# A two-layer decoder trunk on one core: value products gathered, MLP chunks interleaved, gates moved behind later queries

## The chip, the cores and the metric

The kernel runs on one core of a Trainium2 chip. The metric is the device time of one execution in microseconds; lower is better. TensorE (PE) does matrix products into PSUM; its weight loads are listed as PEld. VectorE (DVE), ScalarE (ACT) and GpSimd (POOL) do the elementwise work, and SyncE (SP) issues most DMAs.

## The reference, cut to what matters

Two pre-norm residual layers act on x, 256 tokens by 2048 features, in float32. Layer 0 is grouped-query attention (32 query heads in 4 groups, head dimension 64) over a sliding window of 128 with sinks. Layer 1 is native sparse attention in three branches: compressed keys, selected blocks (with 256 tokens all four blocks are selected) and a window of 512, mixed by sigmoid gates. The compressed keys and values come from a small MLP.

```python
def compress(k, pos, w1, w2):
    blocks = k[:, idx] + pos            # 15 blocks of 32 tokens
    return jax.nn.gelu(blocks @ w1) @ w2
...
    q, kc, vc, ks, vs, kw, vw, gates, z = jnp.split(h @ w_in, ...)
    o = g[0] * o_cmp + g[1] * o_slc + g[2] * o_win
    return (o * jax.nn.silu(z)) @ w_out
```

## The kernel before, in words

**Projections.** The weights stream through in chunks of 128x1024 floats (512 KB), one chunk a step; `steps` holds all of them in order. `load` brings a chunk into one of 4 `raw` buffers four steps ahead. `split`, two steps ahead, makes two float32r parts of it: ACT copies `w_hi`, DVE subtracts to get `w_lo` (3 buffers each). A "tok" step then makes 12 products of 512 columns into the two accumulators `acc0` and `acc1` (one for each half of the tokens), and a "feat" step makes 8 pairs of 512 and 256 columns. A block of 8 tok steps, or two blocks of 4 feat steps, gives 512 output columns, and a `post_...` function takes them out of PSUM. There are 3 PSUM banks with the tag `acc`.

**Order of the steps.** Layer 0 has keys and values, then for each group g its queries (`post_q`) and its gate (`add_z`, `post_z`), then the output projection. Layer 1 has the compressed branch's keys and values (`post_kc`), the selected branch's (`post_kv`), the first MLP (`add_mlp(0)`, 4 chunks of 8 products with 256 columns), the window branch's keys and values, the second MLP (`add_mlp(1)`), the branch gates, then queries and gate of groups 0, 1, 2, 3, then the output projection.

**Attention in the background.** A unit is a group g and a half of the tokens t. Its front transposes the queries, makes scores and softmax; its back transposes the probabilities (`p_transposed`, into `pt` tiles), makes the value products and calls `finalize`. `pipeline` zips the front of one unit with the back of the unit before. After each half step `background` runs pieces of these generators as long as their prices are covered by a credit that grows by `rate` for each half step. A generator that has to wait yields None, which ends that turn.

**The value products.** `pv_pair` makes two products, one for the upper and one for the lower 64 output partitions of the bank `pv`; each is two instructions in the trace, so a pair is four. In layer 1 a unit with t=0 has 2 blocks (so 2 pairs), and one with t=1 has 4. Every pair is issued when the block after it has been transposed. `finalize` waits until the gate of its group is done, multiplies the gate tile `u` by `pv` straight from PSUM, and makes the two parts `aT_hi` and `aT_lo` that the output projection reads.

**The order on the engines.** Nothing is issued when it is called. `Plan.record` collects all operations, and `Plan.order` replays them with estimated prices: on each engine the earliest recorded operation that is ready goes first. The accumulating products get `LAST`, so they fill PE wherever nothing else is ready; the splits get `FIRST`. `together` keeps products side by side on PE. The order that comes out is fixed; on the chip the engines then wait on semaphores. All operations carry the helper's line, L217, so the views are read by tile names.

Of the kernel before, what the change touches and what calls it, by code (L numbers as in the profile page):

```python
# [12 lines left out]
F32 = mybir.dt.float32  # L13
F32R = mybir.dt.float32r
# [6 lines left out]
P = 128  # L21
# [4 lines left out]
NG = 4  # L26
# [313 lines left out]
def trunk(ctx: ExitStack, tc: tile.TileContext, x, final_norm_w, a_w_in, a_w_out, b_w_in, kc_pos, kc_w1, kc_w2, vc_pos, vc_w1, vc_w2,  # L340
# [9 lines left out]
    def acc_bank(name):  # L350
        return pp.tile([P, NB], F32, tag="acc", name=name, bufs=3)
# [10 lines left out]
    def copy(out, in_, scale=1.0):  # L362
        return ACT.activation(out, in_, AF.Copy, scale=scale)
# [272 lines left out]

    def post_q(layer, g):
        def post(t, ps):
            q = sb.tile([P, 2, NB], F32, tag="qs", name="q", bufs=2)[:, 0]
            copy(q, ps, scale=rq[layer][:, t:t + 1])  # L640
            rope(q.rearrange("p (h d) -> p h d", d=HD), t, HPG)
            qs[layer, g, t] = q
            flags.add(("q", layer, g, t))
        return post
# [27 lines left out]

    def post_kv(layer, kT, offs, vt):
        def post(t, ps):
            both = sb.tile([P, 2 * HPG, HD], F32, tag="qs", name="k32", bufs=2)
            k32 = both[:, 0:NG]
            copy(k32.rearrange("p h d -> p (h d)"), ps[:, 0:256], scale=rms[layer][:, t:t + 1])
            DVE.tensor_scalar(vt()[:, t, :], ps[:, 256:512], rms[layer][:, t:t + 1], None, op0=OP.mult)
            rope(k32, t, NG)
            twice = both[:, HPG:2 * HPG].rearrange("p (g a) d -> p g a d", a=2)  # L680
            copy(twice, k32[:, :, None, :].to_broadcast([P, NG, 2, HD]))
            urgent.append(keys_to(kT(), twice, offs[t]))
        return post
# [4 lines left out]
    def post_z(layer, g, part):  # L688
        def post(b, ps):
            if part == b == 0:  # L690
                us[layer, g] = sb.tile([P, 4, S], F32, tag="u", name="u", bufs=2)
            u = us[layer, g][:, 2 * part + b, :]
            side = sb.tile([P, S], F32, tag="q32", name="side", bufs=2)
            copy(side, ps[:, S:2 * S])
            DVE.tensor_tensor(u, ps[:, 0:S], side, op=OP.add)
            if b == 0:
                return
            u = us[layer, g][:, 2 * part:2 * part + 2, :]
            DVE.tensor_tensor(u, u, rbc[:, None, :].to_broadcast([P, 2, S]), op=OP.mult)
            th = sb.tile([P, 2, S], F32, tag="q32", name="th", bufs=2)  # L700
            ACT.activation(th, u, AF.Tanh)
            DVE.scalar_tensor_tensor(u, th, 1.0, u, op0=OP.add, op1=OP.mult)
            if part == 1:
                flags.add(("z", layer, g))
        return post

    def add_z(w, width, col0, layer, g, act):
        for part in range(2):
            add_steps(w, width, col0 + g * NB + part * NB // 2, "feat", act, post_z(layer, g, part))

    def new_aT():
        return (sb.tile([P, KT, S], F32R, tag="aT_hi", name="aT_hi"),
                sb.tile([P, KT, S], F32R, tag="aT_lo", name="aT_lo"))

    def finalize(layer, g, t, pv, aT):
        while ("z", layer, g) not in flags:
            yield None
        u = us[layer, g][:, :, t * P:(t + 1) * P]
        DVE.tensor_tensor(u, u, pv, op=OP.mult)
        hi = aT[0][:, 4 * g:4 * g + 4, t * P:(t + 1) * P]  # L720
        copy(hi, u)
        DVE.tensor_sub(aT[1][:, 4 * g:4 * g + 4, t * P:(t + 1) * P], u, hi)
        flags.add(("a", layer, g, t))
        yield 0.0
# [6 lines left out]
            copy(out, in_)  # L731

    def pt_tile():
        return sb.tile([P, 4, P], F32, tag="pt", name="pt", bufs=4)

    def pv_pair(pv, v, pts, first, last):
        plan.together([PE.matmul(pv[par * HD:(par + 1) * HD], v, pts[par], start=first, stop=last)
                       for par in range(2)])

    def a_scores(g, t, kT, qT, par, sm, nm, den):  # L740
        n = (t + 1) * P
# [53 lines left out]

    def pv_blocks(sms, blocks, pv, close):

        prev = None
        for k, (br, off, v) in enumerate(blocks):
            pts = yield from p_transposed(sms, br, off, k)  # L800
            if prev:
                pv_pair(pv, *prev, prev_first, False)
                yield 900.0
            prev, prev_first = (v, pts), k == 0
        pv_pair(pv, *prev, prev_first, close)
        yield 900.0

    def zip_pieces(a, b):

# [24 lines left out]
    def a_back(g, t, vt, sms, aT):  # L834
        pv = pv_bank()
        gs = slice(g * HD, (g + 1) * HD)
        if t == 0:
            yield from pv_blocks(sms, [(0, 0, vt[:, 0, gs])], pv, True)
        else:
            pts = [[], []]  # L840
            for par in range(2):
                tb = t_bank("pT")
                for i in range(4):
                    PE.transpose(tb[:, i, :], sms[par][0][:, i, 0:P], ident)
                for k in range(2):
                    pt = pt_tile()
                    DVE.tensor_tensor(pt, tb, part[:, k, None, :].to_broadcast([P, 4, P]), op=OP.mult)
                    pts[k].append(pt)
                yield 440.0
            for k in range(2):  # L850
                pv_pair(pv, vt[:, 1 - k, gs], pts[k], k == 0, k == 1)
                yield 900.0
        yield from finalize(0, g, t, pv, aT)

    def pipeline(units, front, back):
# [101 lines left out]
    def post_kc(t, ps):  # L957
        if t == 0:
            b_tiles()
        s = sb.tile([P, 2 * NG, 2, HD], F32, tag="qs", name="kcdup", bufs=2)  # L960
        DVE.tensor_scalar(s, ps.rearrange("p (a d) -> p a d", d=HD)[:, :, None, :].to_broadcast([P, 2 * NG, 2, HD]),
                          rms[1][:, t:t + 1], None, op0=OP.mult)
        urgent.append(kc_gen(t, s))
# [45 lines left out]

    def mlp_tail(kind, ps):  # L1010
        H = room(CH)
        copy(H[0:122], ps[0:122, 0:CH])
        yield 0.0
        tb = t_bank("hid")
        for ut in range(2):
# [15 lines left out]
        copy(c32, tb[0:60, 0, 0:HD])  # L1031
        yield 220.0
        if kind == 0:
            s = sb.tile([P, 1024], F32R, tag="qs", name="cstack", bufs=2)[0:60, 0:256].rearrange(
                "p (a b d) -> p a b d", a=2, b=2)
            src = c32[:, None, :].to_broadcast([60, 2, HD])
            copy(s[:, 0], src)
# [10 lines left out]
        else:  # L1048
            yield 0.0
            tb = t_bank("vsel")  # L1050
            for g in range(NG):
                for b in range(2):
                    PE.matmul(tb[b * HD:(b + 1) * HD, g, 0:HD], mlp["sel"][:, g, :], c32, start=True, stop=True)
            vh = sb.tile([P, 1024], F32R, tag="qs", name="vh", bufs=2)[:, 0:256].rearrange("p (g d) -> p g d", g=NG)
            copy(vh, tb[:, :, 0:HD])
            for b in range(2):
                for hl in range(2):
# [6 lines left out]
            yield 900.0  # L1064
            flags.add("vcmp")

    def add_mlp(kind):
        box = {}

        def mk(i):  # L1070
            st = Step()
            st.cols = 1024
            st.dma = w_dma(W1[kind][0], i * 4 * P, 4, 0, CH, CH)

            def half(b):
                if i == 0 and b == 0:
                    need(("X", kind))
                    box["ps"] = acc_bank("mlp")
                X = mlp["X", kind]
                ps = box["ps"]  # L1080
                for kk in (2 * b, 2 * b + 1):
                    kt = 4 * i + kk
                    for pi, w_ in enumerate((st.hi, st.lo)):
                        PE.matmul(ps[0:122, 0:CH], X[:, kt, :], w_[:, kk * CH:(kk + 1) * CH],
                                  start=kt == 0 and pi == 0, stop=kt == KT - 1 and pi == 1)
                if i == 3 and b == 1:
                    urgent.append(mlp_tail(kind, ps))
            st.halves = [lambda: half(0), lambda: half(1)]
            return st
        for i in range(4):  # L1090
            steps.append(mk(i))
# [43 lines left out]
    def b_add(col, kind, post, before=None):  # L1135
        add_steps(b_w_in[0], B_IN, col, kind, of_hT(hT_b), post, before=before)

    aTB = []
    b_add(2048, "tok", post_kc, before=b_before)
    b_add(2560, "tok", post_kv(1, lambda: lay["kT"], (128, 0), lambda: lay["vs"]))  # L1140
    add_mlp(0)
    b_add(3072, "tok", post_kv(1, lambda: lay["kT"], (272, 400), lambda: lay["vw"]))
    add_mlp(1)
    add_gates()
    for g in range(NG):
        b_add(g * NB, "tok", post_q(1, g))
        add_z(b_w_in[0], B_IN, 3680, 1, g, hT_b)
    nB = len(steps)

    def b_scores(g, t, qT, par, sm, nm, den, sc):  # L1150
# [71 lines left out]
    def b_back(g, t, ctx_):  # L1222
# [13 lines left out]
        tb = t_bank("pcT", F32R)  # L1236
        for i in range(4):
            PE.transpose(tb[:, i, :], pc[:, 2 * i:2 * i + 2].rearrange("p a b c d -> p (a b c d)"), identr)
        pcT = sb.tile([P, 4, P], F32R, tag="pt", name="pcT", bufs=4)
        copy(pcT, tb.bitcast(F32))  # L1240
        yield 230.0
        yield 0.0
# [60 lines left out]
    hT_pair(0, hT0, 0)  # L1303
    for i in range(AHEAD):
        split(steps[i])
    rates = [(0, 450.0), (nA, 900.0), (nA + 8, 600.0), (nA_out, 700.0), (nB, 1200.0)]
    for i, st in enumerate(steps):
        for start, r in rates:
            if i == start:
# [77 lines left out]
```

## Time and profile before

| | before |
|---|---|
| median of 3 runs | 786.74 us (786.48 to 786.99) |
| the profiled execution | 786.12 us, its span 784.4 us |
| granted TensorE clock, mean | 0.998 |
| PE busy | 769.8 us, 98% of the span |
| DVE busy | 561.3 us, 72% |
| ACT busy | 465.8 us, 59% |
| POOL busy | 121.7 us, 16% |

Busy times of PE overlap with the drain of each product, so a product of 512 columns is listed as 0.39 us long while products start about every 0.23 us. The time that a piece of PE work costs is read from start to start.

### The profile page before, as it was taken

To read this page: it belongs to the slowest core of one execution; us is meant where nothing else is said; L and a number is where in the kernel's file an instruction comes from. 1 tells how busy PE (TensorE), PEld (TensorE's weight loads), DVE (VectorE), ACT (ScalarE), POOL (GpSimd) and SP (SyncE) were. 2 spreads that over 40 slices of the span, in tenths; PEclk is the share of its full clock that TensorE was granted. 3 is DMA by queue.
4 is the path that set the end of the run, shared out by engine and by line. 5 is a ranking of instruction groups with operands and counts; after the bars stand their busy time and mean duration, and the time that the engine had idled before them with its cause. 6 is when DMAs were issued, how large, how long until landed. Compare 5 with 4: busy or idle time off the path is not lost.

```text
span 784.4 us, 11578 instructions
## 1 busy us (share of the span) xinstructions
PE 769.8 (98%) x3988; PEld 621.3 (79%) x3988; DVE 561.3 (72%) x1159; ACT 465.8 (59%) x940; POOL 121.7 (16%) x170
## 2 busy tenths in 40 slices
PE   8999999999999999999999999999999999999995
PEld 5888788788787888888788887787778768768884
DVE  6649859779589555566756489769949879965562
ACT  6857557466475544445746486577557758744442
POOL 1111213023022000020101102121111031111110
PEclk9999999999999999999999999999999999999999
DMA  9763654564544565665767653444534453355642
GB/s 326 239 201 121 188 162 136 165 183 134 170 153 155 168 195 183 186 199 162 221 200 217 180 161 108 134 136 113 153 103 128 146 139 108 113 183 171 199 168 107
DMA packets 86474, 129.73 MB, mean 165 GB/s; under 512 B 6322, under 2 KB 43233, under 8 KB 86288
## 3 DMA queue, kind: packets, MB, share of 16 engines
q1 hardware_dynamic: 85648, 127.16, 53.3%
q0 software_dynamic: 336, 1.29, 0.4%
q8 instruction: 31, 0.51, 0.3%
q10 hardware_dynamic: 432, 0.56, 0.2%
q14 instruction: 27, 0.22, 0.1%
HBM read 126.89 MB, written 2.10 MB: 164 GB/s over the span
## 4 chain that ended last, share of the span: by engine, by line
PE 90%; DVE 4%; issue 2%; ACT 1%; DMA 1%; POOL 1%; ACTq 0%; POOLq 0%; DVEq 0%
PE acc L217 74%; PE pv L217 5%; PE s L217 4%; PE pT L217 4%; DVE sm L217 1%; DVE w_lo L217 1%; PE qT L217 1%; ACT w_hi L217 1%; PE xT L217 1%; DMA raw<-in_a_w_in 1%; PE gates L217 1%; DVE u L217 0%; PE pcT L217 0%; POOL rope L217 0%; PE mlp L217 0%
## 5 line engine op out<-in xcount | busy, mean ns | idle before, releaser
L217 DVE TENSOR_TENSOR w_lo<-raw,w_hi 128x1024 fp32r<-128x1024 f32 (+1 forms) x231 | 292.8, 1270 | 159.3 <-ACT w_hi L217 152.3
L217 ACT ACTIVATE w_hi<-raw 128x1024 fp32r<-128x1024 f32 (+1 forms) x231 | 241.5, 1049 | 188.9 <-PE acc L217 150.7
L217 PE MATMUL acc<-w_hi,hT 128*128 128x512 f32 x768 | 243.6, 394 | 1.6 <-ACT w_hi L217 1.6
L217 PE MATMUL acc<-hT,w_hi 128*128 128x512 f32 x512 | 186.2, 398 | 0.0
L217 PEld LDWEIGHTS acc<-w_hi,hT 128*128 128x128 f32 x768 | 141.8, 188 | 34.1 <-ACT w_hi L217 5.3
L217 PE MATMUL acc<-w_lo,hT 128*128 128x512 f32 x384 | 150.7, 394 | 0.0
L217 PE MATMUL acc<-hT,w_lo 128*128 128x256 f32 x512 | 145.0, 285 | 0.0
L217 PEld LDWEIGHTS acc<-hT,w_hi 128*128 128x128 f32 x512 | 96.2, 188 | 22.0 <-issue 4.1
L217 PEld LDWEIGHTS acc<-hT,w_lo 128*128 128x128 f32 x512 | 96.7, 189 | 1.5 <-issue 0.8
L217 PE MATMUL acc<-w_hi,aT_lo 128*128 128x512 f32 x236 | 92.4, 391 | 0.0
L217 PE MATMUL acc<-w_hi,aT_hi 128*128 128x512 f32 x236 | 92.1, 392 | 0.0
L217 PE MATMUL acc<-w_lo,aT_hi 128*128 128x512 f32 x236 | 92.0, 391 | 0.0
L217 PEld LDWEIGHTS acc<-w_lo,hT 128*128 128x128 f32 x384 | 72.2, 188 | 16.4 <-issue 2.4
L217 ACT ACTIVATE sm<-sm,nmb 128x128 f32<-128x128 f32 (+1 forms) x128 | 56.8, 444 | 17.9 <-DVE nmb L217 15.7
L217 PEld LDWEIGHTS acc<-w_lo,aT_hi 128*128 128x128 f32 x236 | 44.3, 188 | 11.3 <-issue 2.4
L217 PEld LDWEIGHTS acc<-w_hi,aT_hi 128*128 128x128 f32 x236 | 44.3, 188 | 9.7 <-ACT w_hi L217 0.8
L217 PEld LDWEIGHTS acc<-w_hi,aT_lo 128*128 128x128 f32 x236 | 44.3, 188 | 8.9
L217 POOL TENSOR_TENSOR sm<-sm,denb 128x512 f32<-128x512 f32 (+1 forms) x16 | 28.8, 1798 | 140.9 <-DVE denb L217 71.4
L217 DVE CUSTOM_DVE_ANT_0 sm<-s,mask 128x128 f32<-128x128 f32 (+1 forms) x128 | 43.7, 349 | 9.2 <-PE s L217 9.0
L217 PEld LDWEIGHTS pT<-ident,sm 128*128 128x128 f32 x256 | 30.0, 140 | 13.7 <-issue 5.4
L217 PE MATMUL pT<-ident,sm 128*128 128x128 f32 x256 | 38.8, 276 | 1.2 <-DVE sm L217 0.8
L217 PE MATMUL s<-kTB,qT 128*128 128x272 f32 x192 | 37.8, 292 | 0.0
(186 smaller groups left out, 854.9 us busy)
## 6 DMA issues: line engine op xcount, KB each, us to landing
raw<-in_b_w_in SPq DMA_DIRECT2D x88, 512.0 KB, 3.7
raw<-in_a_w_in SPq DMA_DIRECT2D x71, 512.0 KB, 3.7
raw<-in_a_w_out SPq DMA_DIRECT2D x32, 512.0 KB, 4.4
raw<-in_b_w_out SPq DMA_DIRECT2D x32, 512.0 KB, 4.4
x<-in_x SPq DMA_DIRECT2D x8, 256.0 KB, 6.7
raw<-in_b_cmp_k_w SPq DMA_DIRECT2D x4, 512.0 KB, 3.7
raw<-in_b_cmp_v_w SPq DMA_DIRECT2D x4, 512.0 KB, 4.0
out<-x SPq DMA_DIRECT2D x4, 512.0 KB, 3.2
```

Source lines behind the costliest of these rows:

```text
L217: return getattr(eng.real, method)(*[real(a) for a in args], **{k: real(a) for k, a in kw.items()})
```

## The change

Five things change, and the rest of the diff is buffers that follow from them.

1. `pv_products` takes all blocks of a unit at once, after all of them are transposed; `pt` gets 8 buffers for 4.
2. The 8 MLP chunks alternate with the 8 chunks of the window branch's keys and values (`mixed`); both MLPs share one PSUM bank, a half each.
3. The last gates of layer 1 move: q0 z0 q1 z1 q2 q3 z2 z3 in place of q0 z0 q1 z1 q2 z2 q3 z3.
4. `finalize` no longer waits for a gate: if it isn't done, ACT copies `pv` into a tile `o`, and `gated` runs when the gate is.
5. The rate in layer 1's projections is 750 for 700. Queries get tiles of their own (`q`, 4 buffers), other users of `qs` move to `sm`, and the DMA scratch is set to 8192.

```diff
+            q = sb.tile([P, NB], F32, tag="q", name="q", bufs=4)
...
+                urgent.extend(gated(layer, g, *held) for held in late.pop((layer, g), []))
...
     def finalize(layer, g, t, pv, aT):
-        while ("z", layer, g) not in flags:
-            yield None
+        if ("z", layer, g) not in flags:
+            o = sb.tile([P, NB], F32, tag="q", name="o", bufs=4).rearrange("p (a b) -> p a b", a=4)
+            copy(o, pv)
+            late.setdefault((layer, g), []).append((t, o, aT))
+            yield 0.0
+            return
+        yield from gated(layer, g, t, pv, aT)
+
+    def gated(layer, g, t, pv, aT):
...
+    def pv_products(pv, blocks, close):
+        plan.together([PE.matmul(pv[par * HD:(par + 1) * HD], v, pts[par], start=k == 0,
+                                 stop=close and k == len(blocks) - 1)
+                       for k, (v, pts) in enumerate(blocks) for par in range(2)])
...
     def pv_blocks(sms, blocks, pv, close):
-        prev = None
+        done = []
         for k, (br, off, v) in enumerate(blocks):
             pts = yield from p_transposed(sms, br, off, k)
-            if prev:
-                pv_pair(pv, *prev, prev_first, False)
-                yield 900.0
-            prev, prev_first = (v, pts), k == 0
-        pv_pair(pv, *prev, prev_first, close)
-        yield 900.0
+            done.append((v, pts))
+        yield 0.0
+        pv_products(pv, done, close)
+        yield 800.0 * len(blocks)
...
+                    if kind == 0:
+                        mlp_bank["ps"] = acc_bank("mlp")
...
-    add_mlp(0)
-    b_add(3072, "tok", post_kv(1, lambda: lay["kT"], (272, 400), lambda: lay["vw"]))
-    add_mlp(1)
+    mixed(lambda: b_add(3072, "tok", post_kv(1, lambda: lay["kT"], (272, 400), lambda: lay["vw"])),
+          lambda: (add_mlp(0), add_mlp(1)))
     add_gates()
-    for g in range(NG):
-        b_add(g * NB, "tok", post_q(1, g))
-        add_z(b_w_in[0], B_IN, 3680, 1, g, hT_b)
+    for kind, g in ("q", 0), ("z", 0), ("q", 1), ("z", 1), ("q", 2), ("q", 3), ("z", 2), ("z", 3):
+        if kind == "q":
+            b_add(g * NB, "tok", post_q(1, g))
+        else:
+            add_z(b_w_in[0], B_IN, 3680, 1, g, hT_b)
...
-    rates = [(0, 450.0), (nA, 900.0), (nA + 8, 600.0), (nA_out, 700.0), (nB, 1200.0)]
+    rates = [(0, 450.0), (nA, 900.0), (nA + 8, 600.0), (nA_out, 750.0), (nB, 1200.0)]
...
-    nc = _bacc.Bacc("TRN2", target_bir_lowering=False, num_devices=1)
+    nc = _bacc.Bacc("TRN2", target_bir_lowering=False, num_devices=1, dynamic_dma_scratch_size=8192)
```

## Rows read from the trace of the kernel before

**Rows 1.** The page: busy time of each engine, and the chain that ended last.
```profile
PE 769.8 (98%) x3988; PEld 621.3 (79%) x3988; DVE 561.3 (72%) x1159; ACT 465.8 (59%) x940; POOL 121.7 (16%) x170
...
PE 90%; DVE 4%; issue 2%; ACT 1%; DMA 1%; POOL 1%; ACTq 0%; POOLq 0%; DVEq 0%
```

**Rows 2.** Waits of PE alone: total us, times, longest.
```profile
PE mlp L217 <- DVE w_lo L217: 1.0, 2, 0.5
...
PE pT L217 <- DVE sm L217: 0.8, 3, 0.3
PE kT L217 <- ACT k L217: 0.7, 2, 0.4
```

**Rows 3.** Windows: busy us (instructions) by engine, clock, DMA share, GB/s.
```profile
380.00:422.00 42.00, 40.26 (x232) 33.95 (x231) 26.39 (x32) 25.92 (x40) 7.25 (x16) 1.00 0.72 212
450.00:710.00 260.00, 258.86 (x1435) 203.08 (x1434) 212.50 (x583) 172.15 (x422) 45.88 (x54) 1.00 0.46 132
```

**Rows 4.** Timeline of PE, layer 1: start us, length, form, count in a row.
```profile
509.03 0.62 PE L217 MATMUL acc<-w_hi,hT 128*128 128x512 f32 x2
509.49 0.40 PE L217 MATMUL acc<-w_lo,hT 128*128 128x512 f32 x1
509.81 1.08 PE L217 MATMUL pv<-pt,vw 128*64 128x512 f32 x4
510.82 0.74 PE L217 MATMUL acc<-w_hi,hT 128*128 128x512 f32 x2
511.40 0.40 PE L217 MATMUL acc<-w_lo,hT 128*128 128x512 f32 x1
```

**Rows 5.** Timeline of PE, layer 0, a unit with t=1.
```profile
91.87 0.39 PE L217 MATMUL acc<-w_lo,hT 128*128 128x512 f32 x1
92.18 1.94 PE L217 MATMUL pv<-pt,vA 128*64 128x512 f32 x8
94.05 0.74 PE L217 MATMUL acc<-w_hi,hT 128*128 128x512 f32 x2
94.63 0.40 PE L217 MATMUL acc<-w_lo,hT 128*128 128x512 f32 x1
```

**Rows 6.** The tile pv: its value products in layer 1.
```profile
L217 PE MATMUL pv<-pt,vs x48: 592/618/644, 476.5 to 697.2; 128*64 128x512 f32 x48
...
L217 PE MATMUL pv<-pt,vw x48: 592/618/644, 479.3 to 702.8; 128*64 128x512 f32 x48
```

**Rows 7.** Timeline of PE in the first MLP; in brackets the wait.
```profile
384.51 0.28 PE L217 MATMUL mlp<-w_hi,X 128*122 128x256 f32 x1
385.29 0.38 PE L217 MATMUL mlp<-w_lo,X 128*122 128x256 f32 x1 [0.50 <-DVE w_lo L217]
385.51 0.28 PE L217 MATMUL mlp<-w_hi,X 128*122 128x256 f32 x1
385.62 0.28 PE L217 MATMUL mlp<-w_lo,X 128*122 128x256 f32 x1
```

**Rows 8.** Groups by line, 372 to 425 us: the splits (busy us, mean ns).
```profile
L217 DVE TENSOR_TENSOR w_lo<-raw,w_hi 128x1024 fp32r<-128x1024 f32 x20 | 24.5, 1235 | 15.5 <-ACT w_hi L217 15.5
L217 ACT ACTIVATE w_hi<-raw 128x1024 fp32r<-128x1024 f32 x21 | 21.9, 1057 | 14.3 <-PE acc L217 9.1 <-PE gates L217 2.1 <-DVE room L217 1.6
```

**Rows 9.** Timeline of PE: one wait of keys, one of probabilities.
```profile
390.27 0.66 PE L217 MATMUL kT<-ident,k 128*128 128x128 f32 x4 [0.42 <-ACT k L217]
...
488.52 0.40 PE L217 MATMUL acc<-w_lo,hT 128*128 128x512 f32 x1
489.22 0.66 PE L217 MATMUL pT<-ident,sm 128*128 128x128 f32 x4 [0.31 <-DVE sm L217]
```

**Rows 10.** Groups by line, 450 to 710 us: splits and evacuations.
```profile
L217 DVE TENSOR_TENSOR w_lo<-raw,w_hi 128x1024 fp32r<-128x1024 f32 x62 | 84.3, 1360 | 22.6 <-ACT w_hi L217 19.8 <-PE acc L217 2.3
...
L217 ACT ACTIVATE pt<-pT 128x512 f32<-128x512 f32 x24 | 14.0, 586 | 9.1 <-PE pT L217 9.1
```

**Rows 11.** Chunk loads issued between 372 and 425 us: KB each, median us to landing.
```profile
raw<-in_b_w_in SPq DMA_DIRECT2D x14, 512.0 KB, 4.6
```

More of the change, by code (lines that the diff above doesn't have):

```diff
@@ L638, in post @@
         def post(t, ps):
-            q = sb.tile([P, 2, NB], F32, tag="qs", name="q", bufs=2)[:, 0]
+            q = sb.tile([P, NB], F32, tag="q", name="q", bufs=4)
             copy(q, ps, scale=rq[layer][:, t:t + 1])
@@ L674, in post @@
         def post(t, ps):
-            both = sb.tile([P, 2 * HPG, HD], F32, tag="qs", name="k32", bufs=2)
+            both = sb.tile([P, 2 * HPG, HD], F32, tag="sm", name="k32", bufs=4)
             k32 = both[:, 0:NG]
@@ L713, in new_aT @@
                 sb.tile([P, KT, S], F32R, tag="aT_lo", name="aT_lo"))
+    late = {}
     def finalize(layer, g, t, pv, aT):
-        while ("z", layer, g) not in flags:
-            yield None
+        if ("z", layer, g) not in flags:
[6 more added lines that the diff above has]
+    def gated(layer, g, t, pv, aT):
         u = us[layer, g][:, :, t * P:(t + 1) * P]
@@ L733, in pt_tile @@
     def pt_tile():
[L734 to L738, printed above, removed]
+        return sb.tile([P, 4, P], F32, tag="pt", name="pt", bufs=8)
+    def pv_products(pv, blocks, close):
+        plan.together([PE.matmul(pv[par * HD:(par + 1) * HD], v, pts[par], start=k == 0,
+                                 stop=close and k == len(blocks) - 1)
+                       for k, (v, pts) in enumerate(blocks) for par in range(2)])
     def a_scores(g, t, kT, qT, par, sm, nm, den):
@@ L849, in a_back @@
                 yield 440.0
-            for k in range(2):
-                pv_pair(pv, vt[:, 1 - k, gs], pts[k], k == 0, k == 1)
-                yield 900.0
+            pv_products(pv, [(vt[:, 1 - k, gs], pts[k]) for k in range(2)], True)
+            yield 1600.0
         yield from finalize(0, g, t, pv, aT)
@@ L959, in post_kc @@
             b_tiles()
-        s = sb.tile([P, 2 * NG, 2, HD], F32, tag="qs", name="kcdup", bufs=2)
+        s = sb.tile([P, 2 * NG, 2, HD], F32, tag="sm", name="kcdup", bufs=4)
         DVE.tensor_scalar(s, ps.rearrange("p (a d) -> p a d", d=HD)[:, :, None, :].to_broadcast([P, 2 * NG, 2, HD]),
@@ L1011, in mlp_tail @@
         H = room(CH)
-        copy(H[0:122], ps[0:122, 0:CH])
+        copy(H[0:122], ps[0:122, :])
         yield 0.0
@@ L1033, in mlp_tail @@
         if kind == 0:
-            s = sb.tile([P, 1024], F32R, tag="qs", name="cstack", bufs=2)[0:60, 0:256].rearrange(
+            s = sb.tile([P, 1024], F32R, tag="sm", name="cstack", bufs=4)[0:60, 0:256].rearrange(
                 "p (a b d) -> p a b d", a=2, b=2)
@@ L1053, in mlp_tail @@
                     PE.matmul(tb[b * HD:(b + 1) * HD, g, 0:HD], mlp["sel"][:, g, :], c32, start=True, stop=True)
-            vh = sb.tile([P, 1024], F32R, tag="qs", name="vh", bufs=2)[:, 0:256].rearrange("p (g d) -> p g d", g=NG)
+            vh = sb.tile([P, 1024], F32R, tag="sm", name="vh", bufs=4)[:, 0:256].rearrange("p (g d) -> p g d", g=NG)
             copy(vh, tb[:, :, 0:HD])
@@ L1065, in mlp_tail @@
             flags.add("vcmp")
+    mlp_bank = {}
     def add_mlp(kind):
-        box = {}
         def mk(i):
@@ L1077, in half @@
                     need(("X", kind))
-                    box["ps"] = acc_bank("mlp")
+                    if kind == 0:
+                        mlp_bank["ps"] = acc_bank("mlp")
                 X = mlp["X", kind]
-                ps = box["ps"]
+                ps = mlp_bank["ps"][:, kind * CH:(kind + 1) * CH]
                 for kk in (2 * b, 2 * b + 1):
@@ L1083, in half @@
                     for pi, w_ in enumerate((st.hi, st.lo)):
-                        PE.matmul(ps[0:122, 0:CH], X[:, kt, :], w_[:, kk * CH:(kk + 1) * CH],
+                        PE.matmul(ps[0:122, :], X[:, kt, :], w_[:, kk * CH:(kk + 1) * CH],
                                   start=kt == 0 and pi == 0, stop=kt == KT - 1 and pi == 1)
@@ L1136, in b_add, with mixed @@
         add_steps(b_w_in[0], B_IN, col, kind, of_hT(hT_b), post, before=before)
+    def mixed(add_long, add_short):
+        n0 = len(steps)
+        add_long()
+        n1 = len(steps)
+        add_short()
+        long, short = steps[n0:n1], steps[n1:]
+        del steps[n0:]
+        for i, st in enumerate(long):
+            steps.append(st)
+            if short:
+                steps.append(short.pop(0))
     aTB = []
@@ L1238, in b_back @@
             PE.transpose(tb[:, i, :], pc[:, 2 * i:2 * i + 2].rearrange("p a b c d -> p (a b c d)"), identr)
-        pcT = sb.tile([P, 4, P], F32R, tag="pt", name="pcT", bufs=4)
+        pcT = sb.tile([P, 4, P], F32R, tag="pt", name="pcT", bufs=8)
         copy(pcT, tb.bitcast(F32))
```

## The prediction

> **What bounds the kernel now.** I read the page first. PE is busy for 98% of the span, and the chain that ended last is PE for 90% [rows 1]. So a change that frees DVE, ACT or a queue brings nothing by itself. Only three things can pay: fewer columns on PE, shorter waits of PE, or less time lost where PE passes from one kind of work to another. The change takes away no product, so the first is out.
>
> The waits of PE come next. Apart from the start they are small: the MLP waits for its low weight parts (1.0 us in 2 waits), transposed probabilities for their softmax (0.8 us in 3), transposed keys for ACT (0.7 us in 2) [rows 2]. The listed wait is shorter than what is lost, since the product before still counts as busy while it drains. In one place the view lists 0.31 us, but the starts lie 0.70 us apart where 0.23 is usual [rows 4, 9], so the loss is 0.47, that is 0.16 more than listed. With 0.16 for each wait the three sums are 1.3, 1.3 and 1.0 us.
>
> The third kind can't be seen in busy time, since PE counts as busy throughout. It shows in the timeline, start to start. Accumulating products start every 0.23 us (two from 509.03 to 509.49). Around one pair of value products it goes differently [rows 4]: the last product before it takes 0.32 us until the pair starts, the pair takes 1.01 us until the next product, and the two products after it take 0.58 in place of 0.46. From 509.49 to 511.40 there are 1.91 us, of which three accumulating products explain 0.69; the pair therefore costs 1.22. In layer 0 two pairs stand side by side, and the same stretch, 91.87 to 94.63, takes 2.76 us [rows 5]. Less 0.69 that is 2.07 for two pairs. The second pair so adds only 0.85 (the 1.87 from 92.18 to 94.05 against 1.01 says 0.86). A visit of PE to the value products thus costs 0.36 us on top of the pairs' own 0.86 each, however many pairs it holds.
>
> **The change part by part.**
>
> *Value products in one go.* Layer 1 has 96 such instructions [rows 6], or 24 pairs, and its timeline shows them four at a time with other work between, so there are 24 visits. Afterwards each of the 8 units makes one visit: 4 units of two pairs, 4 of four. 16 visits go. Layer 0 keeps its 8, since its two-pair units are already joined [rows 5]. For the price of a visit the upper bound is 0.36. The lower one counts only the way in and the longer last product: 0.32 - 0.23 = 0.09 and 1.01 - 0.86 = 0.15, together 0.24, which fits if a visit is followed by transposes and not by another accumulating product. I take 0.34, near the upper end, because most visits end like the one in rows 4. 16 x 0.34 = 5.4 us (3.8 to 5.8).
>
> The Trainium skill has a reason for such a price: TensorEngine Tiling (Array Packing), Key Properties, says that changing the tiling mode drains TensorE, and the value products use half the array's columns each. TensorE: Matmul & The Clock Gate, in its part on what happens when you issue a matmul, gives a drain as about 128 cycles; an estimate from it is 0.05 us a switch, 0.11 a visit and 1.7 us for the sum, against the 5.4 that I work out from the rows. The 0.36 that the timeline shows decides.
>
> The other side of this edit: the last block's probabilities must be there before any product of the unit starts, and 8 `pt` buffers are all full then, so the next unit's evacuations wait for the products. In the meantime PE has accumulating products to fill with, as now. Were one unit to wait once, by what the softmax wait costs (0.47 [rows 9]), all 8 would cost 3.8; I take nothing, and keep 2 us either way for waits of this kind, the three present ones (1.3) included.
>
> *MLP chunks alternate.* The MLP needs a split for only 8 short products. They start 0.11 us apart [rows 7], so 8 of them take about 0.9 us; a split takes ACT 1.06 and then DVE 1.24 us [rows 8]. Four chunks in a row outrun the splits, and PE loses 0.78 - 0.11 = 0.67 us at 384.51, twice. Alternating, a pair of steps keeps PE for 12 x 0.23 + 0.9 = 3.7 us, and asks 2.5 of DVE and 2.1 of ACT. The wait goes: -1.3 us, bounds 0 and -1.3. One PSUM bank holds both MLPs, so all three banks are taken during these steps; the third is needed a whole step after its last user was read, so nothing waits there.
>
> *Keys.* The two waits for transposed keys come from the chain ACT, POOL, ACT before them. The chain stays, but what lies beside it on ACT changes. I take half of 1.0: -0.5, bounds 0 and -1.0.
>
> *Late gates, and no waiting.* If a gate isn't done, `finalize` adds an ACT copy of 128x512 from PSUM, 0.59 us by the nearest row [rows 10], at most 16 of them or 9.4 us. ACT is busy 172 of 260 us in this stage [rows 3], and none of its work is in PE's way but the splits, which go first. DVE's multiplication then reads `o` in place of PSUM, same count, same size. The moved steps issue the same products, splits and loads, each from the same queue; only their order changes. I take 0: PE has work all the time in both orders. If the cover were gone, the price would be the third rival's.
>
> *Rate, buffers, scratch.* 0. The rate only moves when background work is recorded. Queries keep 8 KB. The scratch serves POOL's few DMAs, and POOL is busy 16% [rows 1].
>
> **The sum.** 5.4 + 1.3 + 0.5 = 7.2 us. From the profiled execution's 786.12 that gives 778.9. The median of the runs is 0.62 higher, so I forecast 779.5. The bounds together: 5.8 + 1.3 + 1.0 + 2.0 = 10.1 less gives 776.6, and 3.8 + 0 + 0 - 2.0 = 1.8 less gives 784.9.
>
> **The rivals.**
>
> *First: the visits go, but new waits come.* The order on the engines is worked out from estimated prices, and any change shuffles it. PE has 1435 products in the attention stage and waited 1.1 us there [rows 3], which speaks for good filling in any order. Against it: whole units now hang on their slowest evacuation. At two waits of 0.47 a unit, 16 x 0.47 = 7.5 us come back: 787.0, no change. It decides from about 12 such waits, 5.6 us.
>
> *Second: the switch costs only the drain.* If what I read as a visit's price is mostly the draining of products that would show elsewhere, only what the way into a visit costs is saved, 16 x 0.09 = 1.4 us [rows 4]: with MLP and keys 783.5. (The skill's drain, estimated above, would put it near there, at 783.2.) Against it stands that the starts after the visit don't catch up: the two products after it are late by 0.12 more [rows 4].
>
> *Third, slower: DVE becomes the bound at the end.* Groups 2 and 3 now follow each other without a gate block between. DVE works 212.5 us between 450 and 710, of which splits are 84.3 [rows 3, 10]; the rest is 32 us a group. Two groups at the rate of 750 spread over about 46 half steps, 23 splits: 64 + 23 x 1.36 = 95 us of DVE. PE has 23 x 2.73 = 63 us of steps, and for the two groups 2 x (260 - 62 x 2.73) / 4 = 45, so 108. DVE fits if it is busy 88%; its mean is 82% now. At 82% it needs 116 us and is 8 late, and the output projection's first six steps (16 us) don't need group 3, so nothing happens. Were DVE at 70%, 136 us, it would be 28 late, PE would stand for 12, and the time would be 791. It decides from about 24 us of lateness, so I hold it unlikely.
>
> *Fourth: the loads can't follow in the alternating stretch.* 16 chunks of 512 KB in 8 x 3.7 = 29.6 us ask 283 GB/s. Now 212 GB/s take 0.72 of the DMA engines [rows 3], so 283 takes 0.96. A buffer comes round in 4 x 1.85 = 7.4 us, and load (4.6 [rows 11]), ACT and DVE take 6.9. That is close; if each pair of steps came 0.5 us late, 4 us would go: 783.5.
>
> **How the numbers follow.** The forecast, with its own range 776.6 to 782: 0.64. First rival in full 0.07, third 0.06, second 0.08, fourth 0.09; in the remaining 0.06 more waits vanish than I counted and the time falls below 776. This kernel's measurement can tell 0.2%, 1.6 us, from no change, so faster means below 785.2. Forecast, second, fourth and the last case are faster: 0.87. The first rival lies within 0.2%, and the third is slower. For 8 in 10 I take 775.3 to 784.3.
>
> **What would show it.** In the changed profile value products should stand 8 or 16 in a row, 8 visits in layer 1, each with 0.36 us around it; the MLP should show no wait for `w_lo`; PE's waits in the attention stage should stay near 1 us; the last `aT_lo` should come no later against the output projection's first block than now. The prediction is wrong if PE's waits there reach 5 us, if a visit of 16 instructions takes more than 4 x 0.86 + 0.4 us, or if steps at the MLP wait for a DMA.

## The result, and the profile after

The changed kernel takes 782.66 us (median of 5, 782.52 to 783.71) against 786.74 before; the ratio is 0.995 with an interval of 0.9936 to 0.9965. The forecast was 779.5 with a range of 775.3 to 784.3: right in direction and range, 3.2 us too hopeful, and 0.7 us above the narrower range, 776.6 to 782, that I gave to the forecast's own case. A little over half of the forecast gain came (4.1 of 7.2), and the experiments show where the rest stayed: in layer 0, which I had at nothing.

The page after: busy time of each engine, and the chain.

```profile
PE 767.5 (98%) x3988; PEld 624.1 (80%) x3988; DVE 569.7 (73%) x1159; ACT 469.7 (60%) x950; POOL 123.5 (16%) x170
...
PE 83%; DVE 12%; issue 3%; DMA 1%; ACT 0%; ACTq 0%; POOLq 0%; POOL 0%; DVEq 0%
```

PE is as busy as in [rows 1], but the chain now runs through DVE for 12% in place of 4%. That is a sign, not a measure of what is lost: in e7 below, which loses 4.2 us less, it is 3%. The waits of PE:

```profile
PE acc L217 <- ACT w_hi L217: 1.8, 1, 1.8
...
PE acc L217 <- DVE u L217: 1.0, 3, 0.3
PE pT L217 <- DVE sm L217: 0.6, 1, 0.6
PE acc L217 <- DVE kTB L217: 0.3, 1, 0.3
PE pcT L217 <- DVE pc L217: 0.3, 1, 0.3
```

The view leaves out waits under 0.15 us. Those for `w_lo` and for the keys [rows 2] are gone. A new one has come: accumulating products wait for DVE's work on the gate tile `u`. The one put down to `kTB` is a fourth of the same kind: `u<-acc,side` ends just before it there as well.

Since the change takes no product away, the time can be split at five starts of the same evacuations: the last `vA<-acc` (keys of layer 0 done), the first and the eighth `x<-acc` (output projection of layer 0), `room<-gates` (layer 1's branch gates) and the last `x<-acc`. Their rows in the views of the tiles vA, x and gates (count, shortest, median and longest in ns, first and last start), first of the changed kernel:

```profile
L217 DVE TENSOR_SCALAR vA<-acc,r x2: 469/470/472, 35.0 to 35.4; 128x256 f32<-128x256 f32 x2
L217 DVE TENSOR_TENSOR x<-acc,x x16: 683/687/692, 272.1 to 772.8; 128x512 f32<-128x512 f32 x16
L217 ACT ACTIVATE room<-gates x1: 376/376/376, 427.7 to 427.7; 96x256 f32<-96x256 f32 x1
```

and of the kernel before:

```profile
L217 DVE TENSOR_SCALAR vA<-acc,r x2: 469/470/472, 33.8 to 34.2; 128x256 f32<-128x256 f32 x2
L217 DVE TENSOR_TENSOR x<-acc,x x16: 683/692/692, 266.7 to 775.6; 128x512 f32<-128x512 f32 x16
L217 ACT ACTIVATE room<-gates x1: 367/367/367, 425.4 to 425.4; 96x256 f32<-96x256 f32 x1
```

The differences, with the eighth `x<-acc` from the timeline (335.5 before, 340.9 after), and the same for every experiment below:

| kernel | median us | to keys | layer 0 attention | its output | MLP part | layer 1 from its gates |
|---|---|---|---|---|---|---|
| before | 786.74 | 34.2 | 232.5 | 68.8 | 89.9 | 350.2 |
| changed | 782.66 | 35.4 | **236.7** | 68.8 | **86.8** | **345.1** |
| e1 layer 0 waits | 782.90 | 34.6 | 236.8 | 68.7 | 86.9 | 345.0 |
| e2 products only | 792.08 | 34.3 | 236.8 | 68.7 | 90.0 | 350.4 |
| e3 MLP only | 783.82 | 35.3 | 232.6 | 68.7 | 86.9 | 350.6 |
| e4 gates in turn | 786.67 | 35.5 | 236.8 | 68.7 | 86.9 | 349.3 |
| e5 layer 0 as before | 778.52 | 34.3 | 232.6 | 68.7 | 86.9 | 345.1 |
| e6 old pieces only | 779.32 | 35.0 | 232.6 | 68.7 | 86.9 | 345.1 |
| e7 one turn less | 779.36 | 35.2 | 232.5 | 68.8 | 86.8 | 345.1 |
| e8 pairs again | 786.97 | 34.4 | 232.6 | 68.8 | 86.8 | 353.2 |
| e9 both on ACT | 780.38 | 34.5 | 234.2 | 68.7 | 86.9 | 345.2 |
| e10 always wait | 782.66 | 34.5 | 232.6 | 68.7 | 86.9 | 349.5 |
| e11 rate 700 | 778.90 | 35.4 | 232.5 | 68.8 | 86.8 | 344.5 |

So the change brought 3.1 us in the MLP part and 5.1 in layer 1, and lost 4.2 in layer 0. The start up to the keys varies by 1.3 us (34.2 to 35.5), although every engine's instructions stand in the same order there in all these kernels. In the profiled execution of the changed kernel the granted clock of the first 10 us is 0.89, against 1.00 before, so the 1.2 us by which its start is longer are put down to that execution and not to the change. That execution, 783.71, is also the slowest of its five.

**Layer 1.** The visits went as forecast: by the trace there are 24 runs of value products in layer 1 before, of 4 instructions each, and 8 after, four of 8 and four of 16. The timeline of PE at the second unit:

```profile
513.37 0.46 PE L217 MATMUL acc<-hT,w_hi 128*128 128x512 f32 x1
513.76 1.94 PE L217 MATMUL pv<-pt,vs 128*64 128x512 f32 x8
515.53 1.89 PE L217 MATMUL pv<-pt,vw 128*64 128x512 f32 x8
517.35 0.50 PE L217 MATMUL pv<-pcT,vbd 128*128 128x512 f32 x1
```

Sixteen value products stand in a row and take 517.35 - 513.76 = 3.59 us, against 4 x 1.01 for four visits of their own [rows 4]; what each of those cost on the way in and behind it comes on top.

**Layer 0.** The same view, with DVE and ACT and the weight loads (PEld), at the first unit with t=0:

```profile
78.05 1.39 DVE L217 TENSOR_TENSOR u<-u,rbc 128x512 f32<-128x512 f32 x1
...
79.17 2.00 PE L217 MATMUL pv<-pt,vA 128*64 128x512 f32 x4
79.36 0.68 DVE L217 COPY pt<-pT 128x512 f32<-128x512 f32 x1
...
80.09 0.19 PEld L217 LDWEIGHTS pv<-pt,vA 128*64 128x64 f32 x2 [0.73 <-DVE pt L217]
...
81.09 0.66 PE L217 MATMUL pT<-ident,sm 128*128 128x128 f32 x4
```

Four instructions, one pair, take 81.09 - 79.17 = 1.92 us in place of 1.01 [rows 4]. The two products of a pair normally run beside each other, in two halves of the array's columns: in the unit above the instructions of the two halves start 0.007 us apart (513.763 and 513.770 in the trace) and last 0.6 us each. Here the second one, whose instructions start at 80.09 and 80.57, needs probabilities that DVE copies out only at 79.36 to 80.04, behind the gate's multiplication, so its weights are loaded at 80.09 and the halves run one after the other. PE counts as busy throughout: no wait of PE is listed, only one of PEld. Read in the same way, the pairs of the other three groups take 1.52, 1.49 and 1.51; over 1.01 that is 2.4 us in sum. The rest is the new wait, 0.5 us from start to start, once in each group; at group 0:

```profile
87.31 0.39 DVE L217 TENSOR_TENSOR u<-acc,side 128x256 f32<-128x256 f32 x1
...
87.75 0.74 PE L217 MATMUL acc<-w_hi,hT 128*128 128x512 f32 x2 [0.33 <-DVE u L217]
```

The accumulator that the next block needs is read by DVE at 87.31 to 87.70, late, and PE starts 0.72 us after its last product (87.03) in place of 0.23. 2.4 + 4 x 0.5 = 4.4 accounts for the 4.2.

### The profile page after: what moved, and what is told of

Read it like the earlier page. It is cut to its first block, busy times and chain, and to the rows that moved or that the text cites. A ratio compares the mean times of both kernels' runs of the same rounds, so it can differ in the third digit from the quotient of the medians.

```text
span 781.6 us, 11575 instructions
## 1 busy us (share of the span) xinstructions
PE 767.5 (98%) x3988; PEld 624.1 (80%) x3988; DVE 569.7 (73%) x1159; ACT 469.7 (60%) x950; POOL 123.5 (16%) x170
## 4 chain that ended last, share of the span: by engine, by line
PE 83%; DVE 12%; issue 3%; DMA 1%; ACT 0%; ACTq 0%; POOLq 0%; POOL 0%; DVEq 0%
PE acc L217 68%; PE pv L217 4%; DVE w_lo L217 3%; PE s L217 3%; PE pT L217 3%; DVE sm L217 3%; DVE den L217 2%; DVE u L217 1%; PE mlp L217 1%; DVE qT L217 1%; PE qT L217 1%; PE gates L217 1%; PE xT L217 1%; DMA raw<-in_a_w_in 1%; DVE pt L217 1%
## 5 line engine op out<-in xcount | busy, mean ns | idle before, releaser
L217 DVE TENSOR_TENSOR w_lo<-raw,w_hi 128x1024 fp32r<-128x1024 f32 (+1 forms) x231 | 298.6, 1295 | 140.2 <-ACT w_hi L217 137.7
L217 POOL TENSOR_TENSOR sm<-sm,denb 128x512 f32<-128x512 f32 (+1 forms) x16 | 30.5, 1906 | 143.1 <-DVE denb L217 32.3
L217 DVE CUSTOM_DVE_ANT_0 sm<-s,mask 128x128 f32<-128x128 f32 (+1 forms) x128 | 42.6, 347 | 10.1 <-PE s L217 9.6
L217 PEld LDWEIGHTS s<-kTB,qT 128*128 128x128 f32 x192 | 31.9, 188 | 8.2 <-issue 3.1
```

Of the source, the lines that this page charges most:

```text
L217: return getattr(eng.real, method)(*[real(a) for a in args], **{k: real(a) for k, a in kw.items()})
```

## The experiments

**First four: which part lost it.** e1 makes layer 0's hand-over wait again; e2 and e3 put one part of the change into the kernel before; e4 takes the moved gates out.

```diff
 e1
     def finalize(layer, g, t, pv, aT):
+        while layer == 0 and ("z", layer, g) not in flags:
+            yield None
         if ("z", layer, g) not in flags:
 e2, against before: pv_products, pv_blocks, a_back, 8 pt buffers and the scratch of the change, nothing else
 e3, against before: mixed(), add_mlp() with mlp_bank, nothing else
 e4
-    for kind, g in ("q", 0), ("z", 0), ("q", 1), ("z", 1), ("q", 2), ("q", 3), ("z", 2), ("z", 3):
+    for kind, g in ("q", 0), ("z", 0), ("q", 1), ("z", 1), ("q", 2), ("z", 2), ("q", 3), ("z", 3):
```

Expected of e1: 

> The changed kernel, but in layer 0 the hand-over waits for its gate as before (layer 1 keeps the late gates). Theory A: layer 0 lost about 4 us because the backs of its units no longer wait: their work on DVE now lies before the gate's own, so value products and accumulators stand. Then layer 0 goes back to what it was and the time is 778.5 to 779.5. Theory B: layer 0 lost it through the gathered value products themselves (other pieces, 8 buffers): the time stays at 782 to 783.

Measured: 782.90, ratio 0.9953 (0.994 to 0.9967) to before. Layer 0 stays at 236.8. Theory A, the late hand-over, falls.

Expected of e2: 

> The kernel before, with only the value products of a unit in one go (8 buffers, the smaller scratch). Theory A: layer 1 gains 16 visits of 0.34 us and layer 0 stays, 786.7 - 5.4 = 781.3. Theory B: layer 0 loses about 4 us here too, 785.3.

Measured: 792.08, ratio 1.0065 (1.0053 to 1.0078), slower than before. Layer 0 loses the 4.3 us here too, so they come with the gathered products, as theory B says. But layer 1 gains nothing either, 350.4 for 350.2. Neither theory had that. The 8 visits are there; what they save is taken back by new waits of PE, all of these in layer 1:

```profile
PE acc L217 <- ACT aT_hi L217: 1.4, 1, 1.4
PE pT L217 <- ACT pt L217: 1.1, 1, 1.1
PE pT L217 <- DVE pt L217: 0.7, 2, 0.5
```

With four smaller ones they are 4.2 us in 8 waits, against 1.0 in 4 before. With 0.16 for each, as in the prediction, that is some 3.9 us more, so the gathered products themselves save about 3.7 (an estimate). Five of the waits, 3.2 us, stand between 701 and 715 us, around the end of the last unit.

Expected of e3: 

> The kernel before, with only the MLP chunks alternating with the window branch's keys and values, one bank for both. Both theories: the two waits of the MLP go (1.3 us) and those of the keys (1.0 us) go too, as in the changed kernel: 784.1 to 784.7. If the loads can't follow in the alternating stretch it would be 786 or more.

Measured: 783.82, ratio 0.9966 (0.9954 to 0.9979). The MLP part goes from 89.9 to 86.9: 3 us, a little more than the four waits. But for the start, nothing else moves by more than 0.4. The loads follow.

Expected of e4: 

> The changed kernel with q2 z2 q3 z3 as before. If the moved gates cost or bring nothing, 782.0 to 783.4. If moving them spared DVE at the end of layer 1, it gets slower than 784; if it crowded DVE there, faster than 781.5.

Measured: 786.67, ratio 0.9999 (0.9991 to 1.0008); against the changed kernel's 782.66 the moved gates are worth 4.0. It came out on the slower side, in layer 1 (349.3 for 345.1). The timeline of PE at the end of e4's attention:

```profile
705.73 1.89 PE L217 MATMUL pv<-pt,vw 128*64 128x512 f32 x8
707.55 0.49 PE L217 MATMUL pv<-pcT,vbd 128*128 128x512 f32 x1
709.48 0.50 PE L217 MATMUL acc<-w_hi,aT_hi 128*128 128x512 f32 x1 [1.44 <-ACT aT_hi L217]
710.21 0.61 PE L217 MATMUL acc<-w_hi,aT_lo 128*128 128x512 f32 x1 [0.23 <-DVE aT_lo L217]
710.62 0.63 PE L217 MATMUL acc<-w_lo,aT_hi 128*128 128x512 f32 x1
711.05 0.63 PE L217 MATMUL acc<-w_hi,aT_hi 128*128 128x512 f32 x1
...
713.96 0.40 PE L217 MATMUL acc<-w_hi,aT_lo 128*128 128x512 f32 x1
714.20 0.40 PE L217 MATMUL acc<-w_lo,aT_hi 128*128 128x512 f32 x1
```

and windows of e4 around it (columns as in [rows 3], the clock third from the end):

```profile
650.00:700.00 50.00, 49.78 (x279) 40.80 (x277) 46.22 (x138) 33.86 (x94) 9.19 (x7) 1.00 0.47 153
700.00:720.00 20.00, 17.98 (x76) 12.16 (x77) 9.08 (x9) 8.36 (x14) 2.73 (x2) 0.91 0.21 66
```

When the last unit's value products are done, everything else that PE had is done too, and it stands until ACT and DVE have made group 3's parts. By the trace 96 of the output projection's products start before that point in e2, e4 and e10, and the next one waits; in the kernel before it is 76, in the changed one 81, and neither waits. In e4 and e10 PE also comes to the output projection sooner (241.8 and 242.4 us after the branch gates, 247.5 in the changed kernel) and to the end of the last unit later (279.7 and 279.9, against 275.6): less of the attention was done by then. Why it falls behind there was not isolated.

707.55 to 709.48 is 1.93 where 0.23 is usual, so 1.7 us, and the next product comes 0.5 late. Behind the wait products start 0.43 us apart for some 4 us before they are at 0.23 again: the granted clock of the window is 0.91, and for that stretch it is the lower level, 1.2 GHz. The Trainium skill, TensorE: Matmul & The Clock Gate (Part 1: The HAM clock gate), says that the default state is throttled and activity releases it; this row agrees, in that the clock is back after products in a row. The nine products from 710.21 to 713.96 take 3.75 us in place of 2.07. Together that is 3.9 of the 4.2 us by which e4's layer 1 is longer. In e2 the same wait, 1.4 us listed, stands at the same place, but the clock does not fall behind it:

```profile
712.11 0.50 PE L217 MATMUL pv<-pcT,vbd 128*128 128x512 f32 x1
714.05 0.50 PE L217 MATMUL acc<-w_hi,aT_hi 128*128 128x512 f32 x1 [1.44 <-ACT aT_hi L217]
...
715.35 0.39 PE L217 MATMUL acc<-w_hi,aT_hi 128*128 128x512 f32 x1
715.58 0.40 PE L217 MATMUL acc<-w_hi,aT_lo 128*128 128x512 f32 x1
```

So in the executions profiled the lower clock, worth 1.7 us here, followed this wait in e4 and e10 and not in e2.

**Next four: which piece in layer 0.** A background generator hands its turn to the other half of the zip at each yield. The change gives up one more turn (`yield 0.0`) before the value products, and charges a two-pair unit 1600 at once in place of 900 twice.

```diff
 e5 = e6 + the wait of e1
 e6 = e7 +
-            pv_products(pv, [(vt[:, 1 - k, gs], pts[k]) for k in range(2)], True)
-            yield 1600.0
+            for k in range(2):
+                plan.together([PE.matmul(...) for par in range(2)])
+                yield 900.0
 e7, in pv_blocks (close is true in layer 0 alone)
-        yield 0.0
+        if not close:
+            yield 0.0
         pv_products(pv, done, close)
 e8: pv_pair, pv_blocks and a_back of before; the rest as changed
```

In e6 the price of a t=0 unit's products in layer 0 is 900 again too.

Expected of e5: 

> The changed kernel, with layer 0 as it was: its value products in the old pieces (no turn given up before them, a pair with a price of 900 at a time) and the hand-over waiting for its gate; layer 1 as changed. If layer 0's 4 us come from the pieces in which its units are recorded, the time is 778.2 to 779.5. If they come from something else that changed for layer 0 too (8 buffers, own query tiles), it stays at 782 to 783.

Expected of e6: 

> As e5, but layer 0 keeps the late hand-over. By the pieces alone 778.2 to 779.5 again; if pieces and waiting must both be as before, something between 779.5 and 783.

Expected of e7: 

> The changed kernel, and in layer 0 only the turn before the products of a t=0 unit is taken out. If that turn splits the pairs (2.4 us in the trace of the changed kernel), 780.0 to 781.0; if the turn also makes the gate's accumulator late (the four waits of 0.5 us), 778.5; if neither, 782.7.

Measured: 778.52 (0.9896, 0.9883 to 0.991), 779.32 (0.9905, 0.9892 to 0.9919) and 779.36 (0.9906, 0.9892 to 0.9919). All three have layer 0 back at 232.5 or 232.6, and differ only in the start. One `yield 0.0`, run by four units, is the whole loss. The timeline of e7 at the place shown above:

```profile
77.83 0.68 DVE L217 COPY pt<-pT 128x512 f32<-128x512 f32 x1
...
78.72 0.20 PEld L217 LDWEIGHTS pv<-pt,vA 128*64 128x64 f32 x4 [0.25 <-ACT th L217]
78.72 1.08 PE L217 MATMUL pv<-pt,vA 128*64 128x512 f32 x4
...
79.73 0.50 PE L217 MATMUL acc<-hT,w_hi 128*128 128x512 f32 x1
```

The copy is done before the pair starts, all four weight loads stand together, and the pair takes 1.01 us. The four waits for `u` are gone as well.

Expected of e8: 

> The changed kernel with the value products in pairs as before, in both layers; the MLP chunks, the moved gates, the late hand-over and the rate as changed. If the moved gates and the late hand-over bring nothing of themselves, layer 1 gives back 5.4 us and layer 0 regains 4: 784. If they bring the 4 us here that they brought with the gathered products, 780.

Measured: 786.97, ratio 1.0006 (0.9997 to 1.0015). Layer 1 takes 353.2, that is 2.6 more than with pairs and the old order (e3, 350.6). So neither the gathered products (e2, 350.4) nor the moved gates with the late hand-over, the higher rate and the buffers (e8) gain anything in layer 1 alone; together they gain 5.1. The waits of PE in e8's layer 1:

```profile
PE pT L217 <- ACT pt L217: 0.9, 2, 0.4
PE qT L217 <- POOL q L217: 0.5, 2, 0.3
PE pT L217 <- DVE pt L217: 0.5, 2, 0.2
PE s L217 <- DVE sc L217: 0.4, 2, 0.2
PE pT L217 <- DVE sm L217: 0.4, 2, 0.2
```

They are 2.7 us in 10, against 1.0 in 4 in e3; with 0.16 for each that is 2.7 more, which is the 2.6. Why these settings bring the waits with the pairs and not with the gathered products stays open. In layer 1, e8 and the changed kernel differ in the value products alone, by 8.1 us. The changed kernel's waits there are 0.9 us in 2, so by the same reckoning waits explain 3.1 of it, and the 16 visits the other 5.0, or 0.31 each (an estimate).

**Last three: the split pair, the late hand-over, the rate.**

```diff
 e9, in p_transposed (layer 0, t=0 alone): both tiles by ACT, the turn of the change stays
-            evac(par + k, pt, tb)
+            evac(0 if act else par + k, pt, tb)
 e10 = e5, with the wait in both layers
-        while layer == 0 and ("z", layer, g) not in flags:
+        while ("z", layer, g) not in flags:
 e11 = e5, with
-(nA_out, 750.0)
+(nA_out, 700.0)
```

Expected of e9: 

> The changed kernel with its turn before the products, but in layer 0 both probability tiles of a t=0 unit are evacuated by ACT, so no product waits for a DVE copy that stands behind the gate's work. If the split pairs (1.49 to 1.93 us in place of 1.01, four times, 2.4 us) are a cost of their own, 780.3; if the four waits of 0.5 us for the gate's accumulator go too, 778.5; if the loss only moves, 782.7.

Measured: 780.38, ratio 0.992 (0.9906 to 0.9933); layer 0 at 234.2, that is 2.5 less than the changed kernel. With no copy of DVE behind them the four pairs take 1.01 us each. The four waits for `u` go too, and four others come:

```profile
PE pT L217 <- POOL sm L217: 1.2, 4, 0.4
```

From start to start these cost about what the waits for `u` did (1.9 us), so the 2.5 us gained are the split pairs' 2.4. But e9 does not take the pairs out alone: that they are a cost of their own is read from the timelines, and e9's total fits it. The remaining 1.7 are these new waits.

Expected of e10: 

> As e5, and in layer 1 the hand-over waits for its gate too, so no ACT copy of the value bank at all; the gates stay moved. If the late hand-over in layer 1 brings or costs nothing, 778.5. If it is what lets the moved gates work (groups 2 and 3 would otherwise block each other), 781 or more.

Measured: 782.66, ratio 0.9942 (0.9928 to 0.9955). Layer 1 takes 349.5 for 345.1, with e4's wait for `aT_hi` (1.4 us) at the end and the slow products behind it. So the late hand-over in layer 1 is worth 4.4 us (4.1 between the medians of e10 and e5), although ACT makes six more copies there.

Expected of e11: 

> As e5 with the rate in layer 1's projections at 700 as before. If the rate only moves when background work is recorded, 778 to 779; if group 3 then ends too late for the output projection, 780 or more.

Measured: 778.90, ratio 0.9897 (0.9883 to 0.991), not to be told from e5's 778.52. Layer 1 is 0.6 us shorter in e11's profile, the start 1.1 longer; the higher rate brings nothing that shows.

## Why the prediction was right, and where it was not

**Value products in layer 1: right in sum.** I had 5.4 for 16 visits; layer 1 gained 5.1, and a visit of sixteen instructions takes 0.15 us on top of its pairs (3.59 less 4 x 0.86), as one of four does. The second rival, 1.4 us, is out: with waits set aside the visits are worth 3.7 (e2) to 5.0 (e8 against the changed kernel). But the 5.4 did not come by itself: in e2 new waits took it all back, and it took the moved gates and the late hand-over to keep them away. One reading behind the 0.34 was also wrong. I said that most visits end like the one in [rows 4], at an accumulating product; by the trace 10 of the 24 do, and 14 end at transposes or scores, for which my own lower bound, 0.24, was meant.

**MLP and keys: right, but small.** I had 1.3 + 0.5, and 3.1 came. Both waits for keys went, of which I had counted half, and the part shrank by another 0.8 that no listed wait explains. The fourth rival, loads that can't follow, did not occur.

**Late gates: wrong as a price of 0, right in the total.** I treated the moved gates and the late hand-over as edits that cost and bring nothing. Taken out one at a time they are worth 4.2 (e4) and 4.4 us (e10) in layer 1 with the gathered products. The place is the one that I named in the third rival, the output projection's need of group 3. DVE at its limit is not what the rows show there: between 700 and 720 in e4 it is busy for 9.1 of 20 us. PE runs out of other work before the last unit is done, stands, and in these two runs goes on at the lower clock. The slower side of my distribution stood closer than 0.06 says: the gathered products alone made the kernel slower (e2).

**The step that failed: "Layer 0 keeps its 8, since its two-pair units are already joined", and with it "I take nothing" for new waits.** I looked for a gain in layer 0, found none, and put its cost at 0. The edit changes the pieces in which layer 0's work is recorded all the same; the term is +4.2 us. In kind this is the first rival, new waits after a shuffle; I expected it in layer 1, where the units change most, and priced it by listed waits, while more than half of it is a loss that no wait of PE lists. The signs that I named all came out, 8 visits, 3.59 us for sixteen instructions, no wait for `w_lo`, 0.9 us of waits in the attention stage; none of them looks at layer 0. That the total lies well inside the range is in part luck: 1.3 us that I had not counted in the MLP part stand against the 4.2, and without them it would be 784.0, just under the range's end.

## What to carry to other kernels

Where a list of priorities is made by generators that take turns, every yield is part of the schedule: compare the order on each engine for the parts that the edit wasn't meant to touch. Look for lost time in start-to-start distances, not in busy time or listed waits; a pair of products that should run beside each other counts as busy when it runs one after the other. And test edits together as well as alone: in layer 1 the gathered products brought nothing without the rest, the rest lost 2.6 us without them, and together they brought 5.

The version to keep is e5, the change with layer 0's pieces and waits as before: 778.52 us, 1.0% under the kernel before and 4 us under the change.

## What the runs showed of the hardware

Two DVE instructions with two SBUF inputs each stand here while POOL works on SBUF tiles. The timelines of the changed kernel's DVE and, below, POOL, in layer 0:

```profile
76.23 1.26 DVE L217 TENSOR_TENSOR den<-den,es 128x4 f32<-128x4 f32 x1
...
78.05 1.39 DVE L217 TENSOR_TENSOR u<-u,rbc 128x512 f32<-128x512 f32 x1
```

```profile
76.18 1.29 POOL L217 TENSOR_TENSOR sm<-sm 128x512 f32<-128x512 f32 x1 [0.70 <-ACT sm L217]
77.85 1.04 POOL L217 TENSOR_TENSOR sm<-sm,den 128x512 f32<-128x512 f32 x1 [0.38 <-DVE den L217]
```

An addition of 4 elements takes 1.26 us, until POOL's instruction ends (77.47). The gate's multiplication, begun 0.20 after POOL's next one, takes 1.39; in e7, begun at 77.23 as POOL's instruction ends (76.00 to 77.29), it takes 0.68. The Trainium skill, SBUF — State Buffer (SBUF: two separate sides), says that DVE with two SBUF inputs and GpSimd hold a shared port in turn, each for a whole instruction; these rows agree. The same multiplication over the whole run (count, shortest, median and longest in ns), of the changed kernel and of e7:

```profile
L217 DVE TENSOR_TENSOR u<-u,rbc x16: 678/692/1389, 78.0 to 679.9; 128x512 f32<-128x512 f32 x16
L217 DVE TENSOR_TENSOR u<-u,rbc x16: 677/691/694, 77.2 to 675.5; 128x512 f32<-128x512 f32 x16
```

In the changed kernel four of the sixteen, one in each group of layer 0, take 1.39 us, and 8 of its 16 small additions 1.23 to 1.26 where the others take 0.15 to 0.17. A copy `pt<-pT`, which reads PSUM, takes 0.63 to 0.69 whether POOL works or not. Among DVE's instructions between 40 and 275 us, those that take over 1.3 times the shortest of their form are 18.2 us longer than it in sum in the changed kernel, against 10.1 before and 10.1 in e7. So with the one turn DVE's instructions take 8 us more there, and that is part of how the copy in the split pair and the work on `u` came to be late; how much of the 4.2 us it explains was not separated. The prices from which the order is made know nothing of it.
